# Attention's q, k and v tiles paired otherwise, with another order of the seven products

## The chip, the cores and the metric

The kernel runs on one core of a Trainium2 chip. The metric is the device time of one execution in microseconds (us). Engines are named as the profile names them: PE is the matmul engine (TensorE), DVE VectorE, ACT ScalarE, POOL GpSimd, SP the engine that issues nearly all the transfers.

## The reference, cut to what matters

Two decoder layers over 1024 positions with 1024 channels, in float32. The first mixer is a gated MLP, the second dilated attention; each is followed by a squared-ReLU MLP. The change lies in the attention mixer:

```
qkv = (h @ w_qkv).reshape(B, S, 3, 3 groups, 8 heads, 64)
for g, (window, dilation) in enumerate(((128, 1), (512, 4), (2048, 16))):
    s = q_g . k_g over the keys t - j*dilation, scaled, plus a relative bias
    m = max(s); p = exp(s - m); den = sum(p); num = p @ v_g
o = sum over g of num_g * exp(m_g - m_all), over the same sum of den_g
return o @ w_out
```

So 36 projections of 128 columns (q, k and v for 3 groups and 4 pairs of heads) have to be made, and attention over each group and pair of heads needs its q, k and v.

## The kernel before, in words

A **unit** is one pair of heads in one dilation group; there are 12, in group order 1, 2, 0 for each of 4 head pairs. Tile (i, m) is unit i's q (m = 0), k (m = 1) or v (m = 2): 128 columns by 1024 positions, made in two halves of 512 positions. Every float32 product is three fp32r matmuls (high and low parts), so one "product" of a 512-deep block is 4 x 3 = 12 matmuls of 128x512.

**Quads.** Two tiles are projected together by Strassen's scheme in its 7-product form. `quads` lists the pairs of tiles, `seven` makes one pair: seven products `one(p)`, with sums on DVE and ACT between them, and four results that `put_out(tile, half, ...)` hands over. In `put_out(0, ...)` the 0 is the pair's first tile, 1 its second. `first` is the first pair, whose products come in an order of their own since the operands of some are ready later. Results go through `out` to `out_v` (v: a copy or an addition, later transposes on PE and a split by `v_side`) or to `out_qk` (q and k: an addition where the result has two parts, a copy to the high part on ACT, L1169, the low part on DVE, L1170). A product with a bank already in use adds to it; 7 and 4 share one bank, 1 and 2 another, 5 and 3 a third.

**Attention.** `attention` walks the 12 x 4 blocks of the units. For each block: scores (12 matmuls at<-k,q), maxima on DVE (L1265) and exponentials on ACT (L1267), transposes on PE (at<-ident,t), a split on ACT and DVE (tr), values (at<-tr,V), and their evacuation in alternating steps of ACT (L1304) and DVE (L1305) into N. `merge` weights the three groups' results with spread factors (L1422, transposes, L1439 to L1451). PSUM has 8 banks: 3 ("mm") for the projections and 5 ("at") for attention.

**What sets the order.** PE's order is fixed when the program is written out: `Flow` keeps a clock of PE time, `product` calls `flow.pump()` after each three matmuls, and `pump` lets attention's generators emit their next step when their due time has come (`LAT` holds the delays). `flow.until(...)` runs those steps at once until something has been reached, with no projection matmuls between them. ACT's, DVE's, POOL's and SP's queues are ordered by the framework's scheduler from the same program, each strictly in order; a wait on one instruction holds everything behind it on its engine. `out_qk` calls `flow.until` before it allocates a k tile: unit i's k waits until unit i - 1 has emitted its last scores, since the slots are shared.

**Behind the pairs.** When the last pair has begun, `ahead_of_last` loads the stored results and splits the output weights, and at the end reloads the residual h (8 transfers of 512 KB). Then `project_three` (9 matmuls each, mm<-o,whi and wlo) and the first MLP weights (`plain`, r<-in_w_up, split into wp) run beside unit 11's attention, then `project_last`, then the second MLP.

Of the kernel before, what the change touches and what calls it, by code (L numbers as in the profile page):

```python
# [112 lines left out]
def trunk(ctx: ExitStack, tc: tile.TileContext, xT, w_u, w_v, w_o, w_s, b_s, w_qkv, w_bo, rel,  # L113
          w_up, w_dn, w_dl, vecs, onehot, outT):
    nc = tc.nc
    flow = Flow()
# [11 lines left out]
    def temp():  # L128
        return tpool.tile([P, HALF], F32, tag="t", name="t", bufs=NT)
# [304 lines left out]
    def up(layer, q):  # L434
        return lambda i, j: w_up[layer, q, i, j]
# [265 lines left out]
    for tiles in ((0, 1), (2,), (3,), (4, 5, 6, 7)):  # L701
        w = [weight(w_o[m]) for m in tiles]
        for s in range(2):
# [5 lines left out]
            if tiles[-1] == 7:  # L709
                start_terms(sq[s], s, 1, terms)  # L710
                if s == 0:
                    first = [plain(up(0, q)) for q in range(2)]
# [376 lines left out]
    U = []  # L1089
    for hp, g in units:  # L1090
        u = Unit()
# [62 lines left out]
    def out_qk(i, m, s, a, b, over):  # L1154

        u = U[i]
        if m not in u.tiles:
            if m == 1 and i > 0:
                flow.until(lambda: U[i - 1].scored.t is not None)
            u.tiles[m] = [slot((P, S), F32R, f"{'qk'[m]}{e}") for e in range(2)]  # L1160
        hi, lo = (permuted(t, s, u.g) for t in u.tiles[m])
        sc = -0.125 if m == 0 else 1.0
        with tc.high_priority(offset=PRIO):
            if b is not None:
                t = a if over else temp()
                nc.vector.tensor_tensor(t, a, b, op=ALU.add)
                a = t
            a = own(a, u.g)
            nc.scalar.activation(hi, a, AF.Copy, scale=sc)  # L1169
            nc.vector.scalar_tensor_tensor(lo, a, sc, hi.bitcast(F32), op0=ALU.mult, op1=ALU.subtract)  # L1170
        u.out_qk = getattr(u, "out_qk", 0) + 1
        if u.out_qk == 4:
            u.q, u.k = u.tiles[0], u.tiles[1]
            u.qk.t = flow.t
# [9 lines left out]
    def seven(w, x, more, put_out, begun=None, first=False):  # L1184

        def one(p, bank=None):
            new = bank is None
            bank = mm_bank() if new else bank
            product(bank, w[p], x.t[p], p in (2, 3, 4) and not (first and p == 3))
            more()  # L1190
            return bank

        def copied(src):
            t = temp()
            with tc.high_priority(offset=PRIO):
                nc.scalar.activation(t, src, AF.Copy)
            return t

        def plus(x, y, out=None):
            out = temp() if out is None else out  # L1200
            with tc.high_priority(offset=PRIO):
                nc.vector.tensor_tensor(out, x, y, op=ALU.add)
            return out

        if first:
            a = one(1)
            u = copied(a)
            d = one(3)
            plus(u, one(6), u)
            one(2, a)  # L1210
            put_out(0, 0, a)
            e = one(7)
            c22 = plus(u, e)
            f = one(5)
            put_out(1, 1, c22, f, True)
            put_out(0, 1, plus(u, f), d, True)
        else:
            u = one(6)
            if begun:
                begun()  # L1220
            u = copied(u)
            a = one(1)
            plus(u, a, u)
            d = one(5)
            c22 = plus(u, d)
            e = one(7)
            put_out(1, 1, c22, e, True)
            one(2, a)
            put_out(0, 0, a)
            one(3, d)  # L1230
            put_out(0, 1, u, d)
        one(4, e)
        put_out(1, 0, u, e, True)

    def geometry(g, j):

# [278 lines left out]
            h[k] = slot(name=f"h{k}")  # L1515
            nc.sync.dma_start(h[k], hd[k])

    quads = [((1, 1), (1, 2))]
    for i in range(2, NU, 2):
        quads += [((i, 1), (i, 0)), ((i, 2), (i + 1, 0)), ((i + 1, 1), (i + 1, 2))]  # L1520

    flow.add(attention())
    for s in range(2):
# [31 lines left out]
    first = [plain(up(1, 0))]  # L1555
# [108 lines left out]
```

## Time and profile before

| | |
|---|---|
| time, median of 3 | 2153.97 us (2151.77 to 2154.95) |
| the profiled execution | 2152.68 us, of which its span is 2151.0 us |
| PE busy | 2114.8 us (98%), 10242 matmul instructions |
| DVE, ACT, POOL busy | 1636.2, 1121.3, 562.8 us |
| attention's pairs on PE | from about 971 to 1435.5 us, its last unit until about 1479 us |

In a timeline row stand the start, the time from the first start to the last end, the engine, the line in the kernel, output<-inputs, shapes and count, and in brackets the idle time ahead of the row with what ended it. The span of a matmul instruction includes its latency: in a dense run they start every 0.227 us for 512 columns, though each is shown some 0.39 us long. PEclk is the share of PE's full clock that was granted.

### The profile page before, as it was taken

How to read it: one execution, taken by the hardware profiler on the slowest of the kernel's cores; microseconds unless marked ns; L12 is line 12 of the kernel's file. 1: busy time of each engine (PE TensorE's matmuls, PEld its weight loads, DVE VectorE, ACT ScalarE, POOL GpSimd, SP SyncE). 2: the span in 40 equal slices, each digit the busy share in tenths (PEclk: the TensorE clock that was granted, in tenths of full speed). 3: DMA queues.
4: the chain of work that ended last, by engine and by line, in shares of the span. 5: the costliest groups of instructions: out<-in, count | busy, mean ns of one | idle time of the engine just before them, and what ended most of it. 6: DMA issues, size and time to landing. Idle time of an engine off the chain costs nothing.

```text
span 2151.0 us, 30121 instructions
## 1 busy us (share of the span) xinstructions
PE 2114.8 (98%) x10242; PEld 1752.0 (81%) x10242; DVE 1636.2 (76%) x3010; ACT 1121.3 (52%) x2261; POOL 562.8 (26%) x417
## 2 busy tenths in 40 slices
PE   8999999999999999999999999999999999999998
PEld 7888887888878888887888788887888888788887
DVE  7975268567699888897787877877866766988886
ACT  7644136555564444346665666664455556544443
POOL 2100113233223333521212122201133332332345
PEclk9999999999999999999999999999999999999999
DMA  6411113455364444221112111150055543644432
GB/s 223 141 59 50 40 47 134 165 189 184 114 195 153 156 157 137 89 93 37 46 46 56 40 47 47 44 182 27 32 176 195 191 158 123 200 153 141 144 106 78
DMA packets 158813, 247.04 MB, mean 115 GB/s; under 512 B 33481, under 2 KB 47940, under 8 KB 158660
## 3 DMA queue, kind: packets, MB, share of 16 engines
q1 hardware_dynamic: 158336, 244.94, 35.1%
q8 instruction: 80, 1.31, 0.3%
q14 instruction: 73, 0.60, 0.1%
q10 hardware_dynamic: 324, 0.18, 0.0%
HBM read 180.41 MB, written 64.66 MB: 114 GB/s over the span
## 4 chain that ended last, share of the span: by engine, by line
PE 87%; DVE 7%; ACT 2%; DMA 2%; issue 2%; SPq 1%; DVEq 0%; ACTq 0%
PE at L180 43%; PE mm L180 41%; PE at L187 2%; DVE wp L206 1%; DMA t<-hid 1%; DVE hx L206 1%; ACT t L1267 1%; DMA r<-in_w_up 1%; DVE h L935 1%; DVE k L1170 0%; DVE q L1170 0%; ACT wp L205 0%; SPq L169 0%; DVE tr L206 0%; DVE h L338 0%
## 5 line engine op out<-in xcount | busy, mean ns | idle before, releaser
L205 ACT ACTIVATE wp<-r 128x512 fp32r<-128x512 f32 (+3 forms) x490 | 294.2, 605 | 450.8 <-PE at L180 289.1
L180 PE MATMUL at<-hx,wp 128*128 128x512 f32 x1770 | 413.8, 389 | 4.6 <-DVE wp L206 2.6
L206 DVE TENSOR_TENSOR wp<-r,wp 128x512 fp32r<-128x512 f32 (+3 forms) x490 | 376.2, 771 | 38.6 <-ACT wp L205 34.9
L180 PE MATMUL mm<-y,wp 128*128 128x512 f32 x1608 | 399.3, 394 | 2.2 <-ACT t L1127 1.0
L180 PEld LDWEIGHTS at<-hx,wp 128*128 128x128 f32 x1770 | 331.8, 188 | 75.8 <-DVE h L935 3.7
L180 PEld LDWEIGHTS mm<-y,wp 128*128 128x128 f32 x1608 | 300.1, 189 | 68.1 <-DVE h L338 1.6
L180 PE MATMUL at<-t,wp 128*128 128x512 f32 x1344 | 314.0, 389 | 0.0
L180 PEld LDWEIGHTS at<-t,wp 128*128 128x128 f32 x1344 | 252.2, 188 | 52.7 <-DVE t L798 0.4
L408 POOL TENSOR_TENSOR t<-r 128x512 f32<-128x512 f32 (+3 forms) x78 | 112.8, 1446 | 677.8 <-DMA r<-in_w_dn 299.2
L410 POOL TENSOR_TENSOR r<-r 128x512 f32<-128x512 f32 (+3 forms) x77 | 115.0, 1493 | 388.7 <-DVE wp L206 352.7
L180 PE MATMUL mm<-t,wp 128*128 128x512 f32 x768 | 192.9, 399 | 0.0
L206 DVE TENSOR_TENSOR hx<-t,hx 128x512 fp32r<-128x512 f32 x192 | 178.5, 942 | 5.9 <-ACT hx L205 5.9
L180 PE MATMUL mm<-hx,wp 128*128 128x512 f32 x708 | 171.7, 389 | 0.1
L180 PEld LDWEIGHTS mm<-t,wp 128*128 128x128 f32 x768 | 141.4, 189 | 30.1 <-issue 0.2
L267 POOL TENSOR_TENSOR t<-t 128x512 f32<-128x512 f32 (+1 forms) x54 | 71.5, 1325 | 354.6 <-ACT t L258 352.9
L180 PE MATMUL mm<-y,whi 128*128 128x512 f32 x512 | 158.3, 390 | 0.0
L180 PEld LDWEIGHTS mm<-hx,wp 128*128 128x128 f32 x708 | 132.7, 188 | 28.1 <-DVE b L961 0.7
L935 DVE TENSOR_TENSOR h<-h,at 128x512 f32<-128x512 f32 x144 | 97.6, 680 | 55.3 <-PE at L180 55.3
L798 DVE TENSOR_TENSOR t<-t,at 128x512 f32<-128x512 f32 x116 | 79.2, 684 | 77.5 <-PE at L180 77.3
L180 PE MATMUL at<-y,wp 128*128 128x512 f32 x552 | 138.1, 391 | 0.0
L205 ACT ACTIVATE hx<-t 128x512 fp32r<-128x512 f32 x192 | 118.3, 629 | 30.6 <-DMA t<-hid 24.1
L413 POOL TENSOR_TENSOR r<-r 128x512 f32<-128x512 f32 (+3 forms) x77 | 105.4, 1369 | 82.7 <-issue 48.2
(221 smaller groups left out, 3198.8 us busy)
## 6 DMA issues: line engine op xcount, KB each, us to landing
t<-hid SPq DMA_DIRECT2D x194, 256.0 KB, 5.1
hid<-t SPq DMA_DIRECT2D x140, 256.0 KB, 2.5
r<-in_w_up SPq DMA_DIRECT2D x128, 256.0 KB, 2.8
r<-in_w_dn SPq DMA_DIRECT2D x88, 256.0 KB, 2.7
r<-in_w_qkv SPq DMA_DIRECT2D x72, 256.0 KB, 2.6
hid<-b SPq DMA_DIRECT2D x56, 256.0 KB, 2.7
r<-in_w_v SPq DMA_DIRECT2D x48, 256.0 KB, 3.9
h<-in_xT SPq DMA_DIRECT2D x16, 256.0 KB, 3.3
```

Source lines behind the costliest of these rows:

```text
L180: nc.tensor.matmul(out, lhsT, rhs, **kw)
L187: nc.tensor.transpose(out, src, ident)
L205: nc.scalar.activation(hi, src, AF.Copy)
L206: nc.vector.tensor_tensor(lo, src, hi.bitcast(F32), op=ALU.subtract)
L267: nc.gpsimd.tensor_tensor(self.acc, self.acc, sq, op=ALU.add)
L408: tt(r7, r[0, 0], r[1, 0], op=ALU.subtract)
L410: tt(r6, r[1, 0], r[0, 0], op=ALU.subtract)
L413: tt(r3, r[0, 1], r6, op=ALU.subtract)
L798: nc.vector.tensor_tensor(out, x, y, op=ALU.add)
L935: engine.tensor_tensor(hs[i, s], hs[i, s], src, op=ALU.add)
L1267: nc.scalar.activation(p[:, c], p[:, c], AF.Exp, bias=m, scale=-1.0, accum_out=dn)
```

## The change

Four things change, all in attention.

- The pairs: unit i (even) had k with q, then v with the next unit's q, then the next unit's k with v. Now q goes with v, then the next unit's q with k of this one, then the next unit's k with v. The first pair, k and v of unit 1, is turned round: v is its first tile now.
- The products of every pair but the first come as 6, 1, 7, 5, 4, 2, 3 in place of 6, 1, 5, 7, 2, 3, 4. The second tile's halves are handed over after the fourth and the fifth product, the first tile's after the sixth and the seventh. Before, the second tile's came after the fourth and the seventh, the first tile's after the fifth and the sixth.
- In the first pair the order of the products stays; its second tile's half 1 is handed over at the end, after half 0.
- A q tile waits as well, until the unit two ahead of it has emitted its last scores (from unit 2 on); k tiles wait as before.

```diff
         u = U[i]
         if m not in u.tiles:
-            if m == 1 and i > 0:
-                flow.until(lambda: U[i - 1].scored.t is not None)
+            if m < 1 < i or m and i:
+                flow.until(lambda: U[i - 2 + m].scored.t is not None)
             u.tiles[m] = [slot((P, S), F32R, f"{'qk'[m]}{e}") for e in range(2)]
...
             e = one(7)
             c22 = plus(u, e)
             f = one(5)
-            put_out(1, 1, c22, f, True)
             put_out(0, 1, plus(u, f), d, True)
         else:
             u = one(6)
...
             u = copied(u)
             a = one(1)
             plus(u, a, u)
+            e = one(7)
+            c22 = plus(u, e)
             d = one(5)
-            c22 = plus(u, d)
-            e = one(7)
-            put_out(1, 1, c22, e, True)
+            put_out(1, 1, c22, d, True)
+        one(4, e)
+        put_out(1, 0, u, e, first)
+        if first:
+            put_out(1, 1, c22, f, True)
+        else:
             one(2, a)
             put_out(0, 0, a)
             one(3, d)
-            put_out(0, 1, u, d)
-        one(4, e)
-        put_out(1, 0, u, e, True)
+            put_out(0, 1, u, d, True)
...
-    quads = [((1, 1), (1, 2))]
+    quads = [((1, 2), (1, 1))]
     for i in range(2, NU, 2):
-        quads += [((i, 1), (i, 0)), ((i, 2), (i + 1, 0)), ((i + 1, 1), (i + 1, 2))]
+        quads += [((i, 0), (i, 2)), ((i + 1, 0), (i, 1)), ((i + 1, 1), (i + 1, 2))]
```

PE has the same 10165 matmul instructions of the program before and after. Their order is the same up to the first values of unit 0 (987.7 us in the profiled execution before) and again from about 1479 us on, so what moves lies in some 491 us. Three places follow.

PE, first pair: unit 0's first values (at<-tr,V), the transposes and the scores (at<-k,q) of its later blocks; mm<-t,wp are products of the first pair. Before:

```order
L180 MATMUL at<-k_8534,q_8531 128x256 x2
L180 MATMUL at<-tr,V 128x256 x2
L180 MATMUL at<-tr,V 128x128 x2
L180 MATMUL at<-tr,V 128x256 x2
L180 MATMUL at<-tr,V 128x128 x2
L187 MATMUL at<-ident,t 128x128 x6
L180 MATMUL at<-k_8534,q_8530 128x128 x2
L180 MATMUL at<-k_8535,q_8530 128x128 x2
```

and now:

```order
L180 MATMUL at<-k_8534,q_8531 128x256 x2
L180 MATMUL mm<-t_8725,wp 128x512 x3
L180 MATMUL mm<-t_8738,wp 128x512 x3
L180 MATMUL mm<-t_8760,wp 128x512 x3
L180 MATMUL mm<-t_8763,wp 128x512 x3
L180 MATMUL mm<-t_8766,wp 128x512 x3
L180 MATMUL mm<-t_8769,wp 128x512 x3
L180 MATMUL mm<-t_8772,wp 128x512 x3
L180 MATMUL at<-tr,V 128x256 x2
L180 MATMUL at<-tr,V 128x128 x2
L180 MATMUL at<-tr,V 128x256 x2
L180 MATMUL at<-tr,V 128x128 x2
```

Between the scores of a block of unit 0 and the next values there stand 21 projection matmuls now (15 before the values after those), where there was none.

PE, start of unit 3 (and of unit 9, with the same rows): values of unit 2's last block, scores of unit 3's first, then transposes of the merge's spread factors and of unit 3's v, all on attention's five banks. Now:

```order
L180 MATMUL at<-tr,V 128x128 x2
L180 MATMUL at<-k_10026,q_9674 128x128 x2
L180 MATMUL at<-k_10027,q_9674 128x128 x2
L180 MATMUL at<-k_10026,q_9675 128x128 x2
L180 MATMUL at<-k_10026,q_9674 128x256 x2
L180 MATMUL at<-k_10027,q_9674 128x256 x2
L180 MATMUL at<-k_10026,q_9675 128x256 x2
L187 MATMUL at<-ident,t 128x128 x12
L180 MATMUL mm<-y,wp 128x512 x3
```

Before, 21 projection matmuls and the transposes of two tiles stood between those values and those scores; now the scores and twelve transposes follow the values at once, and the last four need the bank from which the values have to be evacuated.

ACT, unit 11: its exponentials (t,st), the splits of its transposed blocks (p<-at) and of MLP weights (wp<-r). Before:

```order
L1267 ACTIVATE t,st_14032<-t,st_14032 128x256 x5
L1407 ACTIVATE f<-f 128x24
L1117 ACTIVATE V<-at 128x4x2x64
L205 ACTIVATE p<-at 128x384 x2
L1267 ACTIVATE t,st_14032<-t,st_14032 128x256 x2
L205 ACTIVATE p<-at 128x512 x2
L1267 ACTIVATE t,st_14032<-t,st_14032 128x256
L205 ACTIVATE wp<-r 128x512 x2
```

and now:

```order
L1269 ACTIVATE t,st_14036<-t,st_14036 128x256 x5
L205 ACTIVATE wp<-r 128x512
L1409 ACTIVATE f<-f 128x24
L205 ACTIVATE wp<-r 128x512 x3
L205 ACTIVATE p<-at 128x384 x2
L205 ACTIVATE wp<-r 128x512
L205 ACTIVATE p<-at 128x512 x2
L1269 ACTIVATE t,st_14036<-t,st_14036 128x256 x3
```

Four splits of weights stand ahead of the splits of unit 11's first block now; before, those came first and the weights later. (Lines from 1155 on are numbered up to two higher in the changed kernel.) On SP's queue these four weights' loads are issued behind the eight transfers of h; before, three of the weights were loaded ahead of h.

## The prediction

> **What bounds the kernel now.** I read the page first, then windows over the stretch in which PE's order changes, then PE's waits there, and timelines of the places that these pointed to.
>
> ```profile
> PE 2114.8 (98%) x10242; PEld 1752.0 (81%) x10242; DVE 1636.2 (76%) x3010; ACT 1121.3 (52%) x2261; POOL 562.8 (26%) x417
> PE 87%; DVE 7%; ACT 2%; DMA 2%; issue 2%; SPq 1%; DVEq 0%; ACTq 0%
> ```
>
> PE carries the chain, and no matmul is added or removed. So the change can only give back time in which PE waits or runs at a lower clock, or add such time. How much there is, stage by stage (columns: window, its length, busy time and count of PE, PEld, DVE, ACT, POOL, granted clock, DMA share, GB/s):
>
> ```profile
> 987.70:999.20 11.50, 9.94 (x54) 7.23 (x52) 7.66 (x28) 8.23 (x26) 0.00 (x0) 0.67 0.21 68
> 999.20:1211.50 212.30, 209.16 (x1252) 176.07 (x1251) 166.04 (x437) 132.26 (x353) 42.89 (x30) 0.99 0.17 45
> 1211.50:1225.80 14.30, 11.85 (x61) 9.46 (x60) 14.01 (x33) 6.99 (x17) 4.53 (x3) 0.88 0.06 20
> 1225.80:1437.70 211.90, 209.17 (x1239) 175.58 (x1237) 168.40 (x416) 133.87 (x349) 34.48 (x24) 1.00 0.22 60
> 1437.70:1470.50 32.80, 30.40 (x194) 24.98 (x194) 29.99 (x97) 21.95 (x61) 0.00 (x0) 0.93 0.59 206
> 1470.50:1479.20 8.70, 8.70 (x41) 7.26 (x41) 6.68 (x10) 2.19 (x5) 0.00 (x0) 0.86 0.01 3
> ```
>
> Idle PE time sums to 491.5 - 479.2 = 12.3 us. The missing clock, (1 - clock) x length, is 3.8 + 2.1 + 1.7 + 0 + 2.3 + 1.2 = 11.1 us. Those 23.4 us are all that can be won. They sit in three places: unit 0 (first row), the middle near 1218, and unit 11 (the last two rows). What PE waits for in that stretch (total, times, longest):
>
> ```profile
> PE at L180 <- DVE tr L206: 3.5, 4, 1.1
> PE at L180 <- DVE q L1170: 2.4, 3, 1.0
> PE at L187 <- ACT t L1422: 2.1, 1, 2.1
> PE at L180 <- DVE V L1118: 1.1, 1, 1.1
> PE at L180 <- ACT q L1169: 0.9, 3, 0.4
> ...
> PE at L180 <- DVE k L1170: 0.7, 1, 0.7
> ```
>
> **Unit 0: the uncovered stretch.** The first pair's first tile is k of unit 1. Its first result, after four products, runs into the wait for unit 0's last scores, so unit 0's blocks are written out with nothing between them:
>
> ```profile
> 987.66 0.39 PE L180 MATMUL at<-tr,V 128*128 128x256 f32 x1
> 989.09 1.02 PE L180 MATMUL at<-tr,V 128*128 128x256 f32 x7 [1.04 <-DVE tr L206]
> ...
> 995.67 2.06 PE L187 MATMUL at<-ident,t 128*128 128x128 f32 x6
> ...
> 999.24 6.29 PE L180 MATMUL mm<-t,wp 128*128 128x512 f32 x21
> 1005.36 0.28 PE L180 MATMUL at<-tr,V 128*128 128x256 f32 x1
> ...
> 1117.39 1.04 PE L180 MATMUL at<-tr,V 128*128 128x256 f32 x8
> 1118.26 0.84 PE L187 MATMUL at<-ident,t 128*128 128x128 f32 x6
> 1119.03 0.95 PE L180 MATMUL at<-k,q 64*128 64x128 f32 x12
> 1119.91 3.06 PE L180 MATMUL mm<-y,wp 128*128 128x512 f32 x12
> ...
> 1400.03 5.60 PE L180 MATMUL mm<-y,wp 128*128 128x512 f32 x24
> 1405.47 3.57 PE L180 MATMUL mm<-t,wp 128*128 128x512 f32 x15
> ```
>
> The rows from 1117.39 are the same work in unit 3, between projections: values, transposes and scores take 1119.91 - 1117.39 = 2.52 us a block. Two blocks would be 5.0 us; here (two rounds of the three) they took 999.24 - 987.66 = 11.6 us. That is 6.5 us lost. The 21 matmuls behind them took 1005.36 - 999.24 = 6.1 us; at the pace of the last two rows, (1405.47 - 1400.03) / 24 = 0.227 us each, they would take 4.8: 1.4 us more at the low clock. In the changed kernel v of unit 1 comes first and k's result at the end of the pair, and 21 and 15 projection matmuls (4.8 and 3.4 us) stand where none stood. The values' split, which PE reached after 1 us, now has over 4. The wait on k of 0.7 (unit 1's scores) goes too, since k is done well before unit 0 is. Term: -(6.5 + 1.4 + 0.7) = **-8.6 us**; bounds -9 (all) and -5 (if half of the low clock stays).
>
> The Trainium skill, "TensorE: Matmul & The Clock Gate", section "Why this matters for your kernels", has the clock fall for idle gaps over about 3 us between bursts. No wait in the list above is longer than 2.1 us and yet the clock fell to 0.67, so this trace doesn't bear that condition out. By the rule these losses would have another cause that may stay; that is the third rival below.
>
> **The middle: q as the last to come.** Before, q completes after the seventh product of the pair (k, q), whose four results all need an addition or a copy on ACT and a low part on DVE; its scores come next:
>
> ```profile
> 1127.27 2.13 DVE L1170 SCALAR_TENSOR_TENSOR k<-t,k 128x512 fp32r<-128x512 f32 x1
> ...
> 1130.56 0.67 DVE L1166 TENSOR_TENSOR t<-t,mm 128x512 f32<-128x512 f32 x1
> ...
> 1132.42 1.13 DVE L1170 SCALAR_TENSOR_TENSOR q<-t,q 128x512 fp32r<-128x512 f32 x1
> ```
>
> and on ACT and PE:
>
> ```profile
> 1131.27 1.12 ACT L1169 ACTIVATE q<-t 128x512 fp32r<-128x512 f32 x1 [0.49 <-DVE t L1166]
> ...
> 1132.44 0.44 PE L180 MATMUL at<-k,q 64*128 64x128 f32 x4 [0.23 <-ACT q L1169]
> 1133.60 0.66 PE L180 MATMUL at<-k,q 64*128 64x128 f32 x8 [0.72 <-DVE q L1170]
> ```
>
> q's chain is 0.67 + 1.12 + 1.13 = 2.9 us, and it starts late because k's low part and others are ahead of it on DVE. Three units pay this, 2.4 + 0.9 = 3.3 us. Now k(i) is handed over after the fourth and fifth product, with only one heavy result ahead of it, and two products (24 matmuls, 5.4 us) between its last product and its scores: 2.9 us and one low part of up to 2.1 fit. I take 0.5 us as what is left: -2.8. The wait on V (1.1) goes with the better spacing, -1.1, and with these waits the low clock of the third window, 1.7: **-5.6 us** in all; bounds 0 (the same queue on DVE delays k as it did q) and -7 (the 1.2 us of idle time left in that window go too).
>
> **New waits.** Unit 3 and unit 9 start with values, scores and twelve transposes in a row. The last four need the bank of the values, which is released after four alternating steps, ACT and DVE, twice:
>
> ```profile
> 1124.85 1.04 PE L180 MATMUL at<-tr,V 128*128 128x256 f32 x8
> ...
> 1129.74 0.38 ACT L1304 ACTIVATE N<-at 64x256 f32<-64x256 f32 x1 [1.20 <-DVE N L1305]
> ...
> 1131.26 0.42 DVE L1305 TENSOR_TENSOR N<-N,at 64x256 f32<-64x256 f32 x1
> ```
>
> Without a queue that is 2 x (0.38 + 0.41) = 1.6 us; in this instance it took from 1125.9 to 1131.7, 5.8 us. Scores and eight transposes cover some 1.2 us of it, so each costs 0.4 to 4.6 us. DVE has k's low part just ahead there, I take 1.3: +2.6. One more bank wait of the kind that the list has (tr, 3.5 in 4) comes at unit 1, where transposes of v follow scores: +0.7. Together **+3.3 us**, bounds +1 and +10.
>
> **Unit 11, the end of attention.** Here less work is left to cover it. On SP, h's transfers stand behind the exchange of unit 10's maxima, and the weights' loads behind h:
>
> ```profile
> 1420.32 0.89 PE L180 MATMUL at<-k,q 64*128 64x128 f32 x12
> ...
> 1425.73 1.23 SPq L1387 DMA_DIRECT2D sc<-st  x2
> 1430.15 0.38 SPq L1389 DMA_DIRECT2D ex<-sc  x1
> 1436.63 4.07 SPq L1516 DMA_DIRECT2D h<-hd  x8
> ...
> 1452.14 1.26 ACT L205 ACTIVATE wp<-r 128x512 fp32r<-128x512 f32 x2 [0.75 <-DMA r<-in_w_up]
> ```
>
> From the last scores of unit 10 to the exchange's second half are 9.8 us, so h can be issued some 10.3 us after them; the first weight loaded behind h was there 15.5 us after h's first issue (1436.63 to 1452.14). In the changed order PE has 66 matmuls of 512 columns (15.0 us) and the small work of some three blocks (2.5 us each), about 22 us, from those scores to the second block's transposes of unit 11, which reuse the banks of the first block's. ACT releases these only behind four weight splits: 10.3 + 15.5 + 4 x 0.6 + 1.1 (a split on both engines) = 29.3 us. PE would stand for up to 7 us; if the loads come 2 us sooner, 5. Before, this stage had 2.4 us idle, 2.1 of it on the factors (L1422), which have time to be ready after the new stall. So +3 to +5 net of that, less what the later work loses no more since ACT has caught up; the missing clock (2.3 + 1.2) may stay or double. I take **+2.6 us**, between 0 (the stall only moves) and +9.
>
> **Sum.** -8.6 - 5.6 + 3.3 + 2.6 = -8.3 us. The profiled execution took 2152.68 us (span 2151.0): 2144.4. The median of the runs is 1.3 above it, so **2145.7 us**. The new bank and transfer waits are covered by nothing; the projections that cover unit 0 are the first pair's own and are taken from nowhere else.
>
> **Rivals.** (1) The end eats the gain. ACT's four weight splits hold PE for 7 us and the clock stays halved for as long as the two low windows did, so this term is +9 and the middle brings half: -8.6 - 2.8 + 3.3 + 9 = +0.9, 2154.9, no change that can be told. For it speaks the fixed order on ACT; against it, that most of this stage was lost before too. (2) The end costs nothing and the middle clears: -9 - 7 + 1 + 0 = -15, 2139. (3) The low clock isn't due to the uncovered blocks and appears as often: the 3.8, 1.4 and 1.7 us stay, -8.3 + 6.9 = -1.4, 2152.6. The rows speak against it, since each low stretch follows a thinned one. (4) Slower: product 4 now starts one product after 7, in 7's bank, which the addition c22 on DVE has to have read. One product covers it, 12 x 0.227 = 2.7 us, where two did before. If that addition ends later than this after product 7, as q's did above (1127 to 1130.56 until its addition started), each pair pays. At 1 us in each of the 16 pairs the sum is -8.3 + 16 = +7.7, 2161.7; it decides from 0.8 us a pair, 12.6 us in all. Against it: no PE wait on an addition (L1202) is in the list, and these run with priority. That the order doesn't change on PE is excluded by the listing.
>
> **How the numbers follow.** What a measurement can tell from no change is 0.2%, 4.3 us: 2149.7 and 2158.3 are the limits. The forecast has 0.50, with 2141 to 2150 as its own range, which stays on the fast side but for its end; (1) 0.20; (2) 0.12; (3) 0.07; (4) 0.11. Faster 0.50 + 0.12, less 0.01 for that end: 0.61; same 0.20 + 0.07 + 0.01 = 0.28; slower 0.11. The range takes in (2), most of it, (1) and (3) and leaves (4) out: 2138 to 2157.
>
> **What would show it.** Unit 0's blocks at about 2.5 us each with the clock at 1.0 until the first pair has ended; the row "DVE q L1170" gone or under 0.5 us; new waits of twelve transposes on N twice; near the end a wait of PE on tr, p or t of 4 us or more, with ACT waiting on r<-in_w_up ahead of it. Waits of mm products on L1202 would mean rival 4; a wait of PE above 8 us at the end, rival 1.

## The result, and the profile after

The changed kernel is **slower by 0.36%**: 2161.05 us median (2157.96 to 2163.48, 8 runs) against 2152.34 (2147.93 to 2154.95, 8 runs on the same chip), ratio 1.0036, 95% interval 1.0026 to 1.0047, which is 5.6 to 10.1 us. The forecast was 2145.7 with a range up to 2157. The profiled execution took 2158.93 us (span 2157.2), at the lower end of its runs; against the span before, 2151.0, that is 6.2 us more.

Busy times and the chain's shares on the page of the changed kernel hardly move:

```profile
PE 2113.3 (98%) x10242; PEld 1750.4 (81%) x10242; DVE 1644.7 (76%) x3011; ACT 1117.9 (52%) x2256; POOL 559.5 (26%) x417
PE 85%; DVE 9%; ACT 3%; issue 1%; DMA 1%; SPq 0%; DVEq 0%; ACTq 0%
```

So the stages have to be read. Windows of the changed kernel (start and end, length, busy time and count of PE, PEld, DVE, ACT, POOL, granted clock, DMA share, GB/s): unit 0's stretch, then four places that the waits below point to.

```profile
987.70:999.20 11.50, 10.91 (x63) 8.79 (x62) 8.41 (x27) 7.05 (x24) 0.00 (x0) 1.00 0.22 68
...
1095.30:1103.00 7.70, 5.10 (x26) 4.27 (x27) 6.76 (x17) 4.88 (x14) 2.35 (x2) 0.78 0.09 34
...
1218.00:1233.00 15.00, 12.47 (x61) 9.91 (x62) 12.98 (x22) 7.83 (x15) 0.00 (x0) 0.89 0.21 72
...
1356.60:1366.00 9.40, 6.79 (x32) 5.52 (x33) 8.15 (x18) 5.92 (x16) 2.35 (x2) 0.82 0.09 31
...
1445.00:1458.00 13.00, 9.50 (x47) 7.29 (x46) 8.81 (x31) 6.48 (x23) 0.00 (x0) 0.74 0.88 350
```

Unit 0 now runs at full clock with 0.6 us idle, where it had 1.6 us idle and a clock of 0.67. But in each of the three windows at 1095, 1357 and 1445 (the starts of units 3, 9 and 11) PE stands for 2.6, 2.6 and 3.5 us and then misses 0.22 x 7.7 = 1.7, 0.18 x 9.4 = 1.7 and 0.26 x 13 = 3.4 us of clock: 15.5 us. At units 3 and 9 the kernel before loses nothing of the kind:

```profile
1095.30:1103.00 7.70, 7.70 (x47) 6.22 (x46) 7.12 (x16) 4.46 (x11) 1.29 (x1) 1.00 0.13 39
1356.60:1366.00 9.40, 9.40 (x62) 7.75 (x60) 8.19 (x20) 5.14 (x15) 2.59 (x2) 1.00 0.03 7
```

At unit 11 it loses elsewhere in the same stretch. PE's waits of the changed kernel from 987 to 1500 (total, times, longest) name what ends it:

```profile
PE at L187 <- DVE N L1307: 5.8, 3, 2.6
PE at L180 <- DVE tr L206: 3.4, 4, 1.6
PE at L180 <- DVE N L1307: 2.7, 1, 2.7
PE mm L180 <- DVE t L1202: 1.8, 1, 1.8
PE at L187 <- ACT t L1269: 1.6, 4, 0.6
PE at L187 <- ACT t L1424: 1.6, 2, 1.4
```

The waits on q (L1170, L1169) and V (L1118) of the list before are gone. In their place stand four waits on N (L1307 is L1305 of before), 8.5 us. The place at unit 3, on PE (start, duration, and in brackets the idle time ahead and who ended it):

```profile
1092.43 1.48 PE L180 MATMUL at<-tr,V 128*128 128x128 f32 x12
1093.84 0.72 PE L180 MATMUL at<-k,q 64*128 64x128 f32 x8
1095.30 0.50 PE L180 MATMUL at<-k,q 64*128 64x256 f32 x4 [0.74 <-DVE k L1170]
1095.73 1.09 PE L187 MATMUL at<-ident,t 128*128 128x128 f32 x8
1099.42 1.09 PE L187 MATMUL at<-ident,t 128*128 128x128 f32 x4 [2.60 <-DVE N L1307]
```

Values, scores and eight transposes are followed by four more, which need the bank of the values. That bank is emptied into N by two copies on ACT and two additions on DVE in turn. The same moments on ACT:

```profile
1095.28 0.63 ACT L1424 ACTIVATE t<-f 128x512 f32<-128x512 f32 x1 [0.97 <-DVE k L1170]
1096.96 0.60 ACT L1196 ACTIVATE t<-mm 128x512 f32<-128x512 f32 x1 [1.05 <-DVE t L1445]
1097.59 0.38 ACT L1306 ACTIVATE N<-at 64x256 f32<-64x256 f32 x1
1098.44 0.38 ACT L1306 ACTIVATE N<-at 64x256 f32<-64x256 f32 x1 [0.48 <-DVE N L1307]
```

on DVE:

```profile
1095.16 1.77 DVE L1445 TENSOR_TENSOR t<-t 128x512 f32<-128x512 f32 x1
1096.86 0.68 DVE L206 TENSOR_TENSOR wp<-r,wp 128x512 fp32r<-128x512 f32 x1
1098.00 0.41 DVE L1307 TENSOR_TENSOR N<-N,at 64x256 f32<-64x256 f32 x1 [0.47 <-ACT N L1306]
1098.85 0.42 DVE L1307 TENSOR_TENSOR N<-N,at 64x256 f32<-64x256 f32 x1 [0.44 <-ACT N L1306]
```

The values were done at 1093.9, N's first copy starts at 1097.6: it stands on ACT behind the copy of product 6 (L1196), which needs a free temporary; the addition of a merge (L1445) holds that one until 1096.9. That addition and a weight's low part (L206) also stand ahead of N's additions on DVE. The rows of unit 9 (1360.73, again 2.60) are the same.

To add this up over attention, each PE instruction was given the median step to its successor for the two kinds of instruction over the profiled runs, and what each stretch took beyond these steps was summed. The stretches are the same instruction numbers in all kernels (from the program's 4300th matmul on, the 4328th PE record of the trace). In us:

| stretch | before | changed | difference | the prediction's term |
|---|---|---|---|---|
| units 0 and 1 (967 to 1061 us) | 17.3 | 11.7 | -5.6 | -8.6 |
| into unit 3 (to 1126) | 5.6 | 10.8 | +5.2 | new waits |
| to 1195 | 6.4 | 4.3 | -2.1 | middle |
| near 1218 (to 1252) | 9.9 | 10.1 | +0.2 | middle |
| to 1335 | 5.9 | 6.0 | +0.1 | |
| into unit 9 (to 1384) | 4.3 | 9.6 | +5.3 | new waits |
| to 1438 | 4.5 | 2.7 | -1.8 | middle |
| unit 11 and the end (to 1521) | 13.7 | 16.7 | +3.0 | unit 11 |
| sum | 67.5 | 71.9 | +4.4 | |

The steps themselves are 1.3 us longer in the changed order (more changes between kinds), so the whole stretch takes 559.7 us in place of 554.0. The other 0.5 of the 6.2 lies outside attention.

### The profile page after: what moved, and what is told of

The parts are those of the page before. It is cut to its first block, busy times and chain, and to the rows that moved or that the text cites. A ratio compares the mean times of both kernels' runs of the same rounds, so it can differ in the third digit from the quotient of the medians.

```text
span 2157.2 us, 30105 instructions
## 1 busy us (share of the span) xinstructions
PE 2113.3 (98%) x10242; PEld 1750.4 (81%) x10242; DVE 1644.7 (76%) x3011; ACT 1117.9 (52%) x2256; POOL 559.5 (26%) x417
## 4 chain that ended last, share of the span: by engine, by line
PE 85%; DVE 9%; ACT 3%; issue 1%; DMA 1%; SPq 0%; DVEq 0%; ACTq 0%
PE at L180 42%; PE mm L180 40%; PE at L187 2%; DVE wp L206 1%; DMA t<-hid 1%; DVE N L1307 1%; DVE t L206 1%; DVE h L338 1%; DVE t L1441 0%; DVE tr L206 0%; DVE k L1170 0%; DVE h L935 0%; ACT wp L205 0%; DVE hx L206 0%; DVE t L1267 0%
## 5 line engine op out<-in xcount | busy, mean ns | idle before, releaser
L206 DVE TENSOR_TENSOR wp<-r,wp 128x512 fp32r<-128x512 f32 (+3 forms) x490 | 373.1, 765 | 42.8 <-ACT wp L205 39.4
L410 POOL TENSOR_TENSOR r<-r 128x512 f32<-128x512 f32 (+3 forms) x77 | 113.7, 1477 | 386.4 <-DVE wp L206 343.3
L206 DVE TENSOR_TENSOR hx<-t,hx 128x512 fp32r<-128x512 f32 x192 | 179.8, 948 | 5.2 <-ACT hx L205 5.1
```

Of the source, the lines that this page charges most:

```text
L206: nc.vector.tensor_tensor(lo, src, hi.bitcast(F32), op=ALU.subtract)
L410: tt(r6, r[1, 0], r[0, 0], op=ALU.subtract)
```

## The experiments

Three theories were put against each other. **A**: the later pairs lose by the waits on N at units 3, 9 and 11 and the low clock behind them, unit 0 gains. **B**: the order of the products costs in every pair. **C**: the pairing itself makes attention late, and what is saved at one place is lost at the next. All runs, ratio to the kernel before on the same chip, and the time from the program's 4300th to its 7400th matmul in the profile (records 4328 to 7452 of PE in the trace; before 554.0, changed 559.7):

| run | median us | ratio (95%) | stretch us |
|---|---|---|---|
| first pair alone | 2153.61 | 1.0002 (0.9993 to 1.0011) | 552.5 |
| first pair old | 2166.81 | 1.0058 (1.0045 to 1.0071) | 566.4 |
| values with priority | 2160.58 | 1.0031 (1.0019 to 1.0043) | 560.2 |
| order, old pairs | 2154.06 | 1.0004 (0.9995 to 1.0012) | 549.9 |
| pairs, old order | 2183.91 | 1.0137 (1.0122 to 1.0153) | 585.8 |
| v later | 2162.05 | 1.0042 (1.0028 to 1.0055) | 568.1 |
| before, v later | 2149.09 | 0.9977 (0.9968 to 0.9986) | 548.4 |
| order, v later | 2158.78 | 1.0029 (1.0018 to 1.0041) | 558.9 |
| v later at 3, 9, 11 | 2159.51 | 1.0032 (1.0020 to 1.0044) | 562.6 |
| no merge addition | 2153.47 | 0.9996 (0.9988 to 1.0005) | 555.6 |
| mixed order, v later | 2153.08 | 1.0000 (0.9991 to 1.0009) | 555.0 |
| before, no merge addition | 2152.63 | 1.0003 (0.9994 to 1.0012) | 553.1 |
| h sooner | 2159.41 | 1.0028 (1.0017 to 1.0039) | 559.2 |
| mixed order to the ninth pair | 2149.99 | 0.9981 (0.9972 to 0.9989) | 551.0 |
| merge addition on POOL | 2160.36 | 1.0032 (1.0020 to 1.0045) | 562.1 |
| own buffer | 2157.09 | 1.0018 (1.0009 to 1.0027) | 557.6 |

### Which part of the change costs

**First pair alone.** Kernel before with:

```
-    quads = [((1, 1), (1, 2))]
+    quads = [((1, 2), (1, 1))]
     (first pair: put_out(1, 1, c22, f, True) moved behind product 4)
```

> Kernel before with only the first pair turned: (v, k) of unit 1 in place of (k, v), so that k's half is handed over at the pair's end; the fifteen later pairs and their product order stay as before. Theory A (unit 0's part gains what was forecast, 8.6 us with bounds 5 and 9; the loss of the changed kernel comes from waits on N's evacuation in the later pairs): about 2152.3 - 8 = 2144 us, 2142 to 2148, and no wait of PE on DVE N over 1 us. Rival B (the product order 7, 5, 4 costs in every pair, the first is indifferent): 2144 to 2152, since this kernel has the old order. Rival C (the first pair's gain is paid back later whatever follows, since the work only shifts): 2152, no difference from before.

No difference, where theory A had 8 us: a miss. Units 0 and 1 go from 17.3 to 15.5 us only. The first stretch is cured, but two of unit 1's blocks now stand one behind the other at 1026, and the clock falls there (window of this run):

```profile
1022.00:1043.00 21.00, 20.23 (x113) 16.47 (x112) 14.93 (x45) 14.60 (x46) 2.67 (x3) 0.92 0.15 28
```

**First pair old.** The changed kernel with the first pair and its hand-over as before.

```
-    quads = [((1, 2), (1, 1))]
+    quads = [((1, 1), (1, 2))]
     (first pair: put_out(1, 1, c22, f, True) back behind product 5)
```

> Changed kernel with the first pair as before: (k, v) of unit 1 and k's half handed over after the fifth product; all later pairs and their order as changed. Theory A: the loss of the later pairs stands alone, 8.7 + 8 = about 17 us over before, 2169 us (2164 to 2173). Rival C (the first pair's gain is paid back later): like the changed kernel, 2161 within 2. The waits on N's evacuation at units 3, 9 and 11 stay under theory A, each 2 us or more.

Slower than before by 0.58%, 12.5 us (9.7 to 15.3), in the range of theory A, with three waits on N of 2.6 to 3.1 us. So the later pairs alone lose about 12 us, and turning the first pair gives back some 5 in their company (1.0058 less 1.0036), not the 8 expected.

**Order, old pairs.** Changed kernel with the old rows of pairs, and with the old wait in `out_qk` (k tiles alone):

```
-        quads += [((i, 0), (i, 2)), ((i + 1, 0), (i, 1)), ((i + 1, 1), (i + 1, 2))]
+        quads += [((i, 1), (i, 0)), ((i, 2), (i + 1, 0)), ((i + 1, 1), (i + 1, 2))]
```

> Old pairing of the later pairs, new order of their products (6, 1, 7, 5, 4, 2, 3 and the halves handed over as in the changed kernel), first pair turned as changed. Beside the kernel with the first pair alone, it shows the order of products by itself. Theory A (the order costs nothing by itself; in the changed kernel the pairing puts values, scores and transposes in a row): within 3 us of the kernel with the first pair alone, about 2144 to 2148. Rival B (product 4 in product 7's bank waits for an addition, or the halves come later, in all 15 pairs, 0.8 us or more each): 2144 + 12 = 2156 or more, with waits of mm products on L1202 in the list.

Within 0.5 us of the run with the first pair alone: the order of products costs nothing by itself, and theory B falls for this pairing. By the profile it moves losses about: 7.4 us in place of 9.9 near 1218 and 9.2 in place of 13.7 at the end, but 8.7 in place of 4.5 ahead of unit 11, by this wait (PE's waits from 1400 to 1480) and 3.4 us of half clock behind it:

```profile
PE at L180 <- ACT tr L205: 2.6, 1, 2.6
```

That the stretch is 4.1 us shorter than before and the median no lower has this reason: the profiled execution (span 2148.0) is the shortest of its runs (2149.69 to 2158.39).

**Pairs, old order.** The changed pairing with the products 6, 1, 5, 7, 2, 3, 4 and the old hand-overs in the fifteen later pairs (edit condensed):

```
-            e = one(7); c22 = plus(u, e); d = one(5); put_out(1, 1, c22, d, True)
+            d = one(5); c22 = plus(u, d); e = one(7); put_out(1, 1, c22, e, True)
+            one(2, a); put_out(0, 0, a); one(3, d); put_out(0, 1, u, d)
```

> New pairing everywhere, but the fifteen later pairs run their products and hand over their halves in the order of the kernel before (6, 1, 5, 7, 2, 3, 4). The pairing by itself. Theory A with the places at which attention's work stands on PE without a projection between: here there are nine such places of 28 instructions or more in the middle of attention (the changed kernel has seven, of the same kinds), among them values, scores and twelve transposes at units 3 and 9 and three doubled blocks. At 5 us each for the two, 7 for unit 11 and 3 for each doubled block the time is 2161 + 3 x 3 = 2170 us, 2163 to 2177. Rival B (the new order of products is what costs): at or under the kernel before, 2145 to 2153.

Slower by 1.4%, 30 us: still more than expected, on the side that A named and against B. PE's waits there, from 985 to 1530, have the same row at the head, twice:

```profile
PE at L187 <- DVE N L1306: 6.7, 2, 4.4
```

So the pairing is what costs, and the new order of products softens it. The new wait of a q tile came and went with the new pairing in these runs, but it holds nothing back: in the lists of pairs the k tile that waits for the same unit's scores is always handed over ahead of it.

### The waits on N

**Values with priority.**

```
+            with tc.high_priority(offset=PRIO):
                 nc.scalar.activation(o, pv[x, c], AF.Copy)
                 nc.vector.tensor_tensor(o, o, pv[r, c], op=ALU.add)
```

> Changed kernel with one edit: the evacuation of the values' bank into N (two copies on ACT, two additions on DVE a block) is scheduled with the same priority as the other evacuations of banks; PE's order is the same. Theory A (the three waits on N's evacuation and the half clock that they set off cost about 5 + 5 + 7 us): if the priority moves these steps ahead of the splits of weights and the sums of products, two thirds of that come back, 2161 - 11 = 2150 us (2145 to 2155). Rival B (product order) and rival C (pairing moves the late halves of k): within 2 us of the changed kernel, 2161. If N's steps stand behind the same additions as before (they wait in order on ACT behind a copy that itself waits for DVE), the time stays too, and the waits on DVE N of 2.6 us stay in the profile: then this run does not tell the two apart.

The time stays, and so do both waits of 2.60. ACT of this run shows why the edit did not reach its aim; N's copy (L1307 here) keeps its place behind L1196:

```profile
1097.79 0.60 ACT L1196 ACTIVATE t<-mm 128x512 f32<-128x512 f32 x1 [1.06 <-DVE t L1446]
1098.41 0.38 ACT L1307 ACTIVATE N<-at 64x256 f32<-64x256 f32 x1
```

So this run does not tell the theories apart.

**v later.**

```
-            yield U[i - 1].pv, 0
+            yield U[i - 1].pv, 3000
```

> Changed kernel with one number of the planner changed: the transposes of the next unit's v are due 3 us after the values of the unit before, not at once. PE does the same instructions, but values, scores and twelve transposes no longer follow each other without projections at units 3 and 9, nor values, scores, transposes and scores at unit 11. Theory A (the three waits on N's evacuation and the half clock behind them are 5 + 5 + 7 us of the loss): no wait of PE on DVE N over 1 us, 2161 - 15 = 2146 us, 2143 to 2151. Rival C (the pairing makes the even units' attention late, and what is taken from one place is lost at the next): 2157 or more, with the waits on other tiles.

The waits on N at units 3 and 9 fall from 2.60 to 1.22 us, and the clock stays full there:

```profile
1097.60:1103.00 5.40, 4.18 (x27) 3.33 (x28) 4.46 (x12) 2.94 (x8) 2.33 (x2) 1.00 0.00 0
1360.20:1366.00 5.80, 4.56 (x29) 3.63 (x30) 4.86 (x12) 3.25 (x9) 2.37 (x2) 1.00 0.01 3
```

The two stretches gain 1.6 and 1.8 us (10.8 to 9.2, 9.6 to 7.8). But the time doesn't fall: theory A's forecast failed, and the result is as theory C has it for this edit. PE's waits from 985 to 1510 have two new heads, k late at 1238 and V late at unit 11:

```profile
PE at L180 <- DVE k L1170: 3.9, 3, 2.4
PE at L180 <- DVE V L1118: 3.8, 1, 3.8
```

The second is the edit's own doing, since it delays V.

**Before, v later.** The same line in the kernel before, as a control.

> Kernel before with the same one number changed as in the run with v's transposes later: a control. The kernel before has no wait on N's evacuation, and its order changes only at the last unit, where scores, transposes and scores then stand in a row. Theory A: 2152 to 2156, no gain, since there was no such wait to take away. If the later transposes gain by themselves, wherever they stand: 2146 or less.

A miss, and a find: 0.23% faster than before (0.14 to 0.32%). The end of attention is where: 9.4 in place of 13.7 us. The windows from 1437.9 to 1487, of this run:

```profile
1437.90:1487.00 49.10, 45.87 (x271) 37.92 (x270) 44.53 (x117) 29.17 (x75) 4.26 (x3) 1.00 0.31 110
```

and of the kernel before:

```profile
1437.90:1487.00 49.10, 46.70 (x266) 38.52 (x265) 41.98 (x116) 26.19 (x69) 0.06 (x1) 0.93 0.39 138
```

The missing clock, 0.07 x 49.1 = 3.4 us, is gone; one wait of 2.1 us on the factors (L1422) became two of 1.2. No wait on N was there to take away.

**v later at 3, 9, 11.**

```
-            yield U[i - 1].pv, 0
+            yield U[i - 1].pv, {3: 3000, 9: 3000, 11: 1500}.get(i, 0)
```

> Changed kernel, v's transposes due later only for units 3 and 9 (3 us) and 11 (1.5 us); elsewhere the order stays. The run with all of them later lost in other places what it gained here (V late at unit 11 by 3.8 us, k late at 1238 us by 2.4). Theory A2 (values, scores and twelve transposes in a row at units 3 and 9 and values, scores, transposes and scores at unit 11 cost what the profile shows there, 5, 5 and 7 us; of the first two a wait on N of 1.2 us stays, since the values still precede the scores): 2161 - 2 - 2 - 5 = 2152 us, 2148 to 2157. Rival C (whatever is moved there is lost at the next place, the pairing leaves too little work between): 2159 or more.

2159.5, in theory C's range. The two places gain 1.5 and 1.8 us as before, and unit 11 gives it back (23.0 in place of 16.7 us), V being 3.5 us late even with the smaller delay.

**No merge addition.** This kernel leaves out one addition of each merge.

```
             if rest is None:
                 rest = t
-            else:
-                nc.vector.tensor_tensor(rest, rest, t, op=ALU.add)
```

> Changed kernel that leaves out one addition on DVE in each of the eight merges (the second scaled part is not added to the first, L1445, 1.77 us where it stands before N's evacuation at unit 3). PE's order is the same. In the changed kernel N's copy on ACT stands behind the copy of product 6, which waits for a buffer that this addition frees; without it that copy waits for k's low part, which ends 1.7 us sooner. Theory A2: the waits on N at units 3 and 9 fall from 2.6 to about 0.9 us and the half clock behind them goes, 3.5 us each, 2161 - 7 = 2154 us, 2151 to 2157. If the wait on N has nothing to do with the buffer, or the clock falls all the same: 2159 to 2161.

2153.47, as expected, with waits on N of 1.45 rather than 0.9 us: on DVE a weight's low part has moved into the slow place. Unit 3 on PE:

```profile
1099.65 1.08 PE L187 MATMUL at<-ident,t 128*128 128x128 f32 x4 [1.45 <-DVE N L1307]
```

By its ratio the run is back at the kernel before. By the profile it gains 4.1 us in attention, of which units 3 and 9 are 2.1; the low clock behind them stayed in that execution.

**Before, no merge addition.** The control.

> Control: the kernel before, leaving out the same addition on DVE in each of the eight merges (L1443 there). Theory A2 (the addition costs time only where it holds the buffer that product 6's copy, and behind it N's copy, waits for, which is in the changed pairing): 2151 to 2154, no difference from before. If the relief of DVE by eight additions of 0.7 to 1.8 us is worth as much anywhere: 2144 to 2147, as much as the 7.6 us that the changed kernel gained by it.

No difference: the eight additions cost time only in the changed pairing. This is the clearest of the comparisons, 0.9996 against 1.0036 with the change and 1.0003 against 1 without it.

**Own buffer.** Nothing is left out; the second part goes to another buffer, so product 6's copy does not wait for the addition.

```
-            t = temp()
+            t = temp() if rest is None else spare()
```

> Changed kernel; the second scaled part of a merge is put into one of the two buffers b in place of a common temporary, so the copy of product 6 no longer waits for the addition L1445 to free it. All work is kept, PE's order is the same, and on DVE the addition and a weight's low part still stand ahead of N's additions. If the buffer is the whole of it: like the run that leaves the addition out, 2151 to 2156, waits on N of 1.5 us or less. If the place of the two operations on DVE ahead of N's additions (1.77 + 0.6 us there) counts as much: N's copy starts 1 us sooner, its additions hardly 0.5 us, waits on N of about 2.1 us and the half clock behind them stay, 2158 to 2161.

The wait is 2.05 us at both places, as expected if the place on DVE counts as much as the buffer (N's copy is early now, but its addition still stands behind the merge's). At unit 3:

```profile
1102.31 0.63 PE L187 MATMUL at<-ident,t 128*128 128x128 f32 x4 [2.05 <-DVE N L1307]
```

The half clock followed at unit 9 and not at unit 3, behind the same wait. Windows of this run behind the two:

```profile
1102.30:1105.70 3.40, 3.39 (x19) 2.92 (x20) 3.40 (x11) 2.85 (x9) 0.07 (x1) 1.00 0.18 67
1359.80:1366.60 6.80, 5.92 (x18) 4.96 (x19) 5.10 (x15) 3.83 (x13) 0.94 (x1) 0.50 0.11 41
```

The time, 2157.09, lies a little under that theory's range and above the other's: the buffer is about half of what leaving the addition out gave (1.0036 to 1.0018 to 0.9996).

**Merge addition on POOL.**

```
-                nc.vector.tensor_tensor(rest, rest, t, op=ALU.add)
+                nc.gpsimd.tensor_tensor(rest, rest, t, op=ALU.add)
```

> Changed kernel with the same addition of the merges moved from DVE to POOL, nothing left out. POOL's additions of 128x512 take 1.3 to 1.5 us in the profile before, so the buffer comes free about when DVE would free it (1096.7), or later if POOL is busy with sums of weights. Theory A2 (the buffer is what N's copy waits for, not DVE's load): about the changed kernel, 2158 to 2163, with the waits on N of 2 us or more. If DVE's load is what counts: like the kernel without the addition, 2152 to 2156.

2160.4, as A2 had it, but not by the wait it named: at unit 3 the stall now falls on k, 1.82 us, since k's low part on DVE takes 2.11 us (1.03 in the changed kernel) while POOL does the addition. DVE of this run:

```profile
1098.32 2.11 DVE L1170 SCALAR_TENSOR_TENSOR k<-t,k 128x512 fp32r<-128x512 f32 x1
1100.34 1.77 DVE L206 TENSOR_TENSOR wp<-r,wp 128x512 fp32r<-128x512 f32 x1
```

and POOL:

```profile
1097.88 1.64 POOL L1445 TENSOR_TENSOR t<-t 128x512 f32<-128x512 f32 x1 [2.52 <-DVE t L1441]
1099.49 2.08 POOL L410 TENSOR_TENSOR r<-r 128x512 f32<-128x512 f32 x1
```

### Unit 11, and versions that combine

In the changed kernel the third wait on N, 2.70 us at 1450.21, has another origin. DVE at that place:

```profile
1445.65 0.69 DVE L338 TENSOR_TENSOR h<-h,mm 128x512 f32<-128x512 f32 x1 [1.13 <-DMA h<-hd]
...
1448.19 0.69 DVE L338 TENSOR_TENSOR h<-h,mm 128x512 f32<-128x512 f32 x1 [0.59 <-DMA h<-hd]
1448.79 0.41 DVE L1307 TENSOR_TENSOR N<-N,at 64x256 f32<-64x256 f32 x1
```

N's additions stand behind additions to h, and these wait for h's transfers.

**h sooner.** `yield 4000` becomes 2000 and `yield 900` twice 600 in the generator that reloads N, the last weights and h; h's transfers then stand ahead of unit 10's exchange on SP.

> Changed kernel with the reloads before the last projection planned sooner (2 us in place of 4 ahead of the splits of N, 0.6 in place of 0.9 between them). PE's order is the same; on SP the eight transfers of h are now issued ahead of the exchange of unit 10's maxima, not behind it. In the changed kernel two of N's additions on DVE stand behind additions to h that wait for these transfers (1.13 and 0.59 us), N's wait there is 2.7 us and 6.8 us of half clock follow. Theory A2: those two waits of DVE on h<-hd go, N's wait falls to 1 us or less, with half of the low clock: 2161 - 4 = 2157 us, 2154 to 2159. Rival C: the exchange is late in its stead, the wait comes back on the factors of the merge: 2160 or more.

2159.4, 0.08% under the changed kernel, which the intervals of the two (1.0017 to 1.0039, 1.0026 to 1.0047) don't tell apart. The waits on h are gone, and the wait on N grew to 6.77 us, on PE:

```profile
1453.60 2.23 PE L180 MATMUL at<-k,q 64*128 64x256 f32 x12 [6.77 <-DVE N L1307]
```

since on ACT N's copy now stands behind weight splits that wait for loads queued behind h:

```profile
1445.88 1.68 ACT L205 ACTIVATE wp<-r 128x512 fp32r<-128x512 f32 x3 [5.52 <-DMA r<-in_w_up]
```

The wait on the factors (L1424, 1.4 us) went for it, so the stretch costs 16.1 in place of 16.7 us. Whichever transfer is last, N's steps stand behind it.

**Order, v later**: the order with old pairs, and 3 us for v.

> First pair turned, old pairing of the later pairs, new order of products, and v's transposes 3 us later: the combination with the fewest places without a projection between (the one after the first pair is gone as well). Theory A: the unit 0 part (5 us by the profiles) stays and the place behind it gains one more: 2147 to 2151, a little under the kernel before. Rival C: 2154 or more, no difference from the kernel with the order alone.

Slower than the order alone by 5 us: the wait at unit 11 (2.3 us on tr) stays and a second of 2.7 us on p comes. A miss.

**Mixed order, v later**: new order in the first twelve later pairs, old in the last three, first pair turned, old pairs, v 3 us later.

> A combination after the profiles of the others: first pair turned; old pairing; the new order of products in the first twelve of the later pairs and the old order in the last three; v's transposes 3 us later everywhere. By the places of the profiles: unit 0 -5, the middle near 1218 -4 (as with the new order and the old pairing), the end of attention -5 (as in the kernel before with v later). If these add: 2152 - 14 = 2138; if half is given back: 2145. I expect 2143, 2138 to 2149. Rival C (gains at one place are lost at the next): 2149 or more, as the kernel before with v later.

No difference from before, 10 us above the forecast. The middle lost its gain (9.5 us near 1218, with a wait of 2.4 us on tr that the order alone did not have).

**Mixed order to the ninth pair**: like the last run, but with the new order in the first nine later pairs and v later for units 10 and 11 only.

> A version that may beat both kernels: first pair turned; old pairing; the new order of products in the first nine of the later pairs, the old in the last six; v's transposes 3 us later for units 10 and 11 alone. From the profiles: up to unit 7 it is the kernel with the new order and old pairing (6.9 us ahead of the kernel before at unit 7), from unit 8 the kernel before with v later (which gains 5 more, the most at the end of attention). If these add 2152 - 12 = 2140, 2138 to 2145. If only the end counts: 2147 to 2149.

0.19% faster than before (0.11 to 0.28%), no better than the kernel before with v later. Both beat the two kernels compared here; neither adds up the gains of its parts.

## Why the prediction was wrong

**Unit 0, -8.6.** The loss named was real: the stretch before took 7.3 us beyond its steps, and the 21 matmuls behind it 1.4. In the profiled execution it went, clock and all. But the term counted the blocks as free in their new place. There they cost about 3 us (waits of 0.61 and 0.64 us on the exponentials, L1269, at 1009 and 1011 us). Net -5.6, inside the bounds. The full clock there is not certain either: in two runs with the same order on PE the half clock came behind these small waits, for 6.8 us from 1011.6 us (own buffer) and for 3.4 us from 1015.1 us (merge addition on POOL), and units 0 and 1 cost about 15 and 13.5 us in place of 11.7.

**Middle, -5.6.** The waits on q and V went. In the three stretches -2.1, +0.2 and -1.8 us remain, -3.7: near 1218 a wait on tr (1.6) and one of a product on L1202 (1.8), with half a clock behind it, took their place.

**New waits, +3.3. This is the step that failed.** The place, the bank and the alternating steps were right, and "DVE has k's low part just ahead there, I take 1.3" was the wrong size: 5.2 and 5.3 us. The working counted one neighbour in the queue on DVE. The runs showed three things that were missing: N's first copy is queued on ACT behind the copy of product 6, which waits for a buffer of the merge; the merge's addition stands on DVE between; and the stall comes with 3.4 us at half clock, up to 1.7 us each, which the term did not price at all. Each place has 2.60 us of wait on N, 0.74 us on k's low part just ahead of it, and this clock. The further +0.7, a bank wait at unit 1, did not come (0.06 us at 1019.3). The two places are 10.5 us, and without this error the sum would have been near the kernel before. The range's upper bound took +10 for this term, but not together with the smaller gains.

**Unit 11, +2.6.** +3.0 by the stretches. The size came out by luck, since the mechanism was only half right: transfers hold PE by way of a queue, but in the changed kernel it is h in front of N's additions, not weights in front of the splits of p. The forecast's stall of up to 7 us behind the weight splits appeared in the run with h sooner.

**Sum.** -5.6 - 3.7 + 10.5 + 3.0 + 1.3 for the longer steps = +5.5 us, against 5.7 in the profile's stretch.

**Rivals.** The slower rival had the right time, 2161.7 (it counted 16 pairs; the order changes in 15), by luck: it has product 4 wait on the addition c22 in every pair, and in the profile one product 4 waited, once, 1.8 us, and the order by itself is free. The low clock at unit 0 did not stay in the profiled execution (third rival). No rival put a wait on N at its price, which is why "slower" had 0.11.

**What stays open.** Leaving the addition out brought the time back to the kernel before, and the control shows that this is bound to the pairing. That the two places alone make up the difference is not shown: of the 8.6 us between those runs (by their ratios) the profiles place 2.1 at units 3 and 9. The two profiled executions differ by 3.4 us only, 2158.93 and 2155.49, one at the lower end of its runs and the other the slowest of its own, so they can't place the rest. The edit that thins these two places and unit 11 alone gave its gain away at unit 11. The pairing delays k of the even units, and delaying v by 1.5 or 3 us moved losses of up to 6 us to other places. A planner's number alone moved the kernel before by 5 us.

## What to carry to other kernels

When a reorder makes a bank the next thing that PE needs, follow the steps that empty it on every engine's queue, and price the whole queue ahead of them, buffers included, not the steps' own 1.6 us. A stall can be paid twice, since the clock may fall with it: here it did so with every wait of PE of 2.6 us or more. And gains found at separate places of such a schedule do not add: two combinations that summed terms of several profiles came out 10 and 15 us above their sums.

## What the runs showed of the hardware

**A DVE operation can be held by POOL.** The addition L1445 of the changed kernel, grouped over its eight instances:

```profile
L1445 DVE TENSOR_TENSOR t<-t x8: 689/694/1772, 1095.2 to 1485.4; 128x512 f32<-128x512 f32 x8
```

It takes 0.69 us, and 1.77 at units 3 and 9. There POOL was at work on a sum of weights:

```profile
1094.44 1.94 POOL L410 TENSOR_TENSOR r<-r 128x512 f32<-128x512 f32 x1 [3.17 <-DVE wp L206]
```

That ends at 1096.38, the addition at 1096.93, 0.55 us later. In the run with the addition on POOL, L206 (1.77 us) ends 0.54 us after POOL's L410, and k's low part 0.91 after POOL's addition. The Trainium skill, "SBUF — State Buffer", section "SBUF: two separate sides", says that a DVE operation with two inputs from SBUF and a GpSimd operation reading SBUF exclude each other for a whole instruction. All three agree, and so does the whole trace of the changed kernel: 177 of DVE's additions and subtractions of 128x512 with both inputs in SBUF lasted over 0.9 us, each of them began while a POOL operation ran, and each ended 0.54 to 0.56 us after it; of the 919 that began with POOL idle none lasted so long. So the 1.1 us by which the addition was late came from an engine with 26% of busy time, and moving it to POOL only made k's low part wait in its stead.

**Half clock comes in pieces.** The low stretches of the changed kernel, by windows:

```profile
1098.90:1102.30 3.40, 2.88 (x12) 2.51 (x12) 3.37 (x11) 2.65 (x9) 0.03 (x1) 0.50 0.02 7
...
1450.50:1457.30 6.80, 6.57 (x24) 5.22 (x24) 4.47 (x21) 5.32 (x19) 0.00 (x0) 0.50 0.86 332
```

They last 3.4 us or twice that, and cost up to half of it. Four of the five came with waits of 2.60, 1.82, 2.60 and 2.70 us. The fifth, from 1505.1 us, came with no wait but behind matmuls of a single column, which the profile shows as busy time:

```profile
1501.02 2.73 PE L180 MATMUL at<-ones,t 128*128 128x1 f32 x24
```

The starts lie on one grid: (1450.5 - 1098.9) / 103 = 3.41 us, and the other three (1228.6, 1361.7, 1505.1) lie on it too. The starts of every run here do so, each execution with an offset of its own.

Between 985 and 1525 us of the 18 profiles all 21 waits of PE of 2.6 us or more came with a low stretch (one that began during the wait or within 3.5 us of its end), 26 of the 46 between 1.3 and 2.5 us did, and none of the 12 between 1.15 and 1.3 us: those of 1.22 in the run with v later had none, those of 1.45 in the run without the addition had one each, and those of 2.05 in the run with its own buffer had one at unit 9 and none at unit 3. Where a wait falls on the grid may decide it; that is not shown. A wait of 1.6 us on tr near 1219 had no low stretch behind it in the changed kernel and in the run with its own buffer, and 3.4 us of it in the run with the addition on POOL, which by itself moves an execution by up to 1.7 us. The rule that the prediction cited from the Trainium skill, "TensorE: Matmul & The Clock Gate", section "Why this matters for your kernels" (gaps over about 3 us), doesn't hold as a bound here: no wait of the changed kernel was that long, and the clock fell five times.
